# Raw weight pieces of the input and output projections loaded two pieces ahead of their split

## The chip, the cores and the metric

The kernel runs on one core of one Trainium2 chip. A core has TensorE (matmul; PE in the profile, its weight load PEld), VectorE (DVE), ScalarE (ACT), GpSimd (POOL) and SyncE (SP). Here SP only issues DMAs, and ScalarE issues some stores. Every engine works its own queue in order. The metric is the device time of one execution in microseconds, the median over several runs.

## What is computed

One encoder layer on x of 1024 tokens by 1024 features, in float32. The reference, cut to what matters:

```python
mod = cond @ w_ada[l] + b_ada[l]                    # cond = silu(c)
sh1, sc1, g1, sh2, sc2, g2 = jnp.split(mod, 6, axis=-1)
h = modulate(rms_norm(x, norm_mix_g[l]), sh1, sc1)
proj = h @ w_in[l]                                  # 1024 x 2832
q_a, k_a, v_a, qk_m, v_m, o_m, gates = jnp.split(proj, splits, axis=-1)
y_attn = axial_gqa_attention(q_a, k_a, v_a, ...)    # 8 heads of 64, 2 key/value heads
y_mem = bidirectional_mlstm(qk_m, v_m, o_m, gates, ...)  # 4 heads of 128, both directions
mix = jnp.concatenate([y_attn, y_mem], axis=-1) @ w_out[l]
x = x + g1[:, None, :] * mix
h = modulate(rms_norm(x, norm_ffn_g[l]), sh2, sc2)
x = x + g2[:, None, :] * ((jax.nn.silu(h @ w_gate[l]) * (h @ w_up[l])) @ w_down[l])
return rms_norm(x, final_norm_g)
```

## The kernel before, in words

Every large product keeps float32 accuracy by splitting both factors into a high and a low part: `whi` and `wlo` of a weight piece, `h_hi` and `h_lo` of the activations. `mm3` (line 311) makes one product of three matmuls: high by high (L312), one cross term (L313) and the other (L314).

**Weight pieces.** All weights that are used as they lie in memory pass through one list, `specs`, of pieces of about 256 KB (128 partitions by 512 columns). Pieces 0 to 11 belong to the first tiles: keys, values, first query tiles, first chunk tile. From piece 12 on come the tiles of the list `IN` (line 47), in that order: the third and fourth query tile (`q` 2 and 3, two pieces each), eight convolution tiles (`f`, two pieces each, weights `w_f`) and three chunk tiles (`t` 2, 1 and 3, four pieces each, weights `w_t`), up to piece 43. Pieces 44 to 75 are the output projection (`o` and `m`, one piece a unit, weights `w_o`), the list `MIX`. From 76 on come the gate and up projections (`w_gu`), and last the down projection.

**A piece's way.** A piece goes through three steps. `raw` (line 443) takes one of three `wst` buffers and issues the DMA on SP; it waits until the piece three before it has been split. `split` (line 461) makes `whi` by a copy on ScalarE and then `wlo` by a subtraction, on GpSimd for most pieces (VectorE for pieces 70 to 79 and a few others). The parts have six buffers each, so that the split of piece i must wait until the matmuls of piece i-6 are done. `load_piece` (line 488) is called once for every piece, when TensorE is done with a piece six before it: in query and convolution tiles (`tile_mms`, line 851) twice in the second half of a tile; in chunk tiles (`chunk_unit`, line 937) four times in the last of eight row blocks, one after the other; in the output projection (`out_unit`, line 1259) after each unit. Before the change it issues the piece's DMA and chains the split behind its arrival. In the down projection (`start["down"]` on) it issues the DMA of the piece `AHEAD` = 2 further on instead.

**Order.** The program is written out by a planner: `Clock` (line 127) runs a small model of the engines and of the DMA queue, chains wait for the times that this model expects, and streams of matmuls (`ck.streams`, line 215) are picked by readiness, main streams before fills. The order of the instructions on every engine is that of the model's time; on the chip each engine then waits for semaphores in that fixed order. SP's queue too is such an order: a store that waits for its data holds up the loads behind it.

**Stages around the change.** From about 84 us the pieces from 12 on are loaded. Up to about 160 us query, key and value tiles are finished: `rope_steps` (line 736) rotates a query tile with `sw` loads and stores it to `q_d`. Then the banks of PSUM are dealt out anew (line 2161) with a single one, `acc`, for the projection's tiles, and attention begins: `att_q` (line 1138) loads a head's queries (`qd`) and splits them (`qs`, low half on GpSimd), `scores` makes S (L1159), VectorE takes the row maximum (`sst`), ScalarE the exponential P, GpSimd the norm, TensorE turns P (L1191), ScalarE and VectorE split it (`PT`), and TensorE multiplies with the values (`av`, L1210). The convolution and chunk tiles fill TensorE between. A convolution tile's halves are evacuated by ScalarE (`xp`), VectorE applies five taps to them (`y`). GpSimd and ScalarE also work off the conditioning products (`ada`). At about 500 us attention ends, and the mLSTM begins (line 2194) with `mk`, `v` and `mq` loads, transposes (L1885, evacuated to `kt`) and `wv` on GpSimd; chunk tile 3 and then the output projection fill in. The gate and up projections begin at about 705 us.

Of the kernel before, what the change touches and what calls it, by code (L numbers as in the profile page):

```python
# [44 lines left out]
AHEAD = 2  # L45
# [204 lines left out]
def layer_kernel(ctx, tc, xT, c, w_ada, vecs, cons, rope, w_f, w_fT, w_t0, w_t, w_o, w_gu, w_d, out):  # L250
# [114 lines left out]
    with tc.manual_schedule():  # L365
# [62 lines left out]
        specs = [first[f][b] for b in range(2) for f in range(3)]  # L428
        start = {("t", 0): [6, 8, 9, 11], ("q", 1): [7, 10]}
# [31 lines left out]
        def split(p, delay, src, shape, *before, lo=None):  # L461

            def split_hi():
                p[0] = lined("whi", shape)
                act.activation(p[0], src(), AF.Copy)

            def split_lo():
                p[1] = lined("wlo", shape)
                (lo or gps).tensor_sub(p[1], src(), p[0].bitcast(F32))

            ck.chain(delay, *before, split_hi, split_lo, flag=p[2])

        made = []

        def piece(i):

            p = [None, None, Flag()]
            made.append((p, Flag(), []))
            if not isinstance(specs[i][0], str):
                src, n, ncol = specs[i][:3]  # L480

                def arrived(st, arrive):
                    made[i][2].append(st)
                    ck.chain(arrive, lambda: None, flag=made[i][1])

                raw([P, n, ncol], src, p[2], arrived)

        def load_piece():

            i = len(pieces)  # L490
            if i == len(specs):
                return
            while len(made) <= min(i + (AHEAD if i + AHEAD >= start["down"] else 0), len(specs) - 1):
                piece(len(made))
            p, there, st = made[i]
            pieces.append(p)
            if isinstance(specs[i][0], str):
                set_piece(p, *specs[i][1])
                return
            split(p, 0.0, lambda: st[0], [P, *specs[i][1:3]], there,  # L500
                  lo=dve if specs[i][3:] == (1,) or i < 9 or start["m", 2] <= i < start["b", 1] else None)
# [91 lines left out]
        def issue():  # L593

            kind, i = loads[0][0], int(loads[0][1:] or 0)
            del loads[0]
            if kind == "x":
                ck.chain(dma(x_t[i], xT[i]), lambda: None, flag=x_at[i])
            elif kind == "a":
                ada_load(i)  # L600
            else:
                load_piece()
            if loads:
                ck.at(max(0.0, ck.dma_t - 5.0 - ck.now), issue)
# [95 lines left out]
        for k in range(KT):  # L700
            if k < PES:
                for n in range(NH):
                    ck.need(sq_ok[k][n])
                    nc.tensor.matmul(msp[n][0], ones, by_pe[k, n], start=k == 0, stop=False)
                    ck.pe(0.86)
            for n in range(NH):
                ck.need(z_ok[k][n])
                for f in range(3):
                    mm3(acc0[f][n][0], weights([f, 3 + f], k, 4), (h_hi[k][:, halves(n)], h_lo[k][:, halves(n)]),
                        k == 0, k == KT - 1)  # L710
                    ck.pe(0.68)
            z_read[k].set(ck, ck.t)
            if k == 3:
                for _ in range(3):
                    load_piece()
            if k == 5:
                for n in range(NH):
                    ck.need(sq_ok[7][n])
                    ms = msp[n][0]
                    nc.tensor.matmul(ms, ones, ssx[n], start=False, stop=True)  # L720
                    ck.pe(0.86)
                    rstd_ok.append(rstd_steps(ms, 1.0 / D, f"n{n}", lambda y, n=n: rstd.__setitem__(n, y)))
                    y_ok.append(ck.chain(0.0, rstd_ok[n], lambda n=n: act.activation(msp[n][0], rstd[n], AF.Copy)))
                for n in range(NH):
                    for i in range(KT):
                        last.append(h_steps(n, i, *last[-3:-2]))
                h_ok = [last[0:KT], last[KT:]]
                ck.chain(0.0, *last[-3:], lambda: None, flag=y_free)
# [122 lines left out]
        def tile_mms(w0, last):  # L851

            for n in range(NH):
                for k in range(KT):
                    yield [pieces[w0 + k // 4][2]] + ([slot("acc")] if k == 0 else [])
                    if k == 0:
                        acc, f = psum_tile([P, HALF], "acc")
                        open_sum[0] = True
                    mm3(acc, weights(w0, k, 4), (h_hi[k][:, halves(n)], h_lo[k][:, halves(n)]), k == 0, k == KT - 1)
                    ck.pe(0.65)  # L860
                    if n == 1 and k % 4 == 3:
                        load_piece()
                    if k == KT - 1:
                        open_sum[0] = False
                        last(n, acc, f)
# [583 lines left out]
        def set_piece(e, p, i, m):  # L1449

            s = 2 * p + i
            R, Q = RAW[s], set_s[s]
            set_p[s][m] = e[2]
            eng = dve if p == 0 else gps
            done = lambda x: [set_p[s][x]] if x in set_p[s] else []
            sh = [P, 4, P]
            if m[0] == "A":
                split(e, 0.0, lambda: R[m[1:]][0], sh, R[m[1:]][1], lo=eng)
            elif m == "S2":
                split(e, 0.0, lambda: Q[2], sh, s2_ok[s], lo=eng)  # L1460
            elif m == "S3":
                split(e, 0.0, lambda: R["11"][0], sh, s2_ok[s], *done("A11"),
                      lambda: dve.tensor_sub(R["11"][0], R["11"][0], R["21"][0]), lo=eng)
            elif m == "S1":
                split(e, 0.0, lambda: Q[1], sh, s2_ok[s], lo=eng)
            else:
                split(e, 0.0, lambda: R["12"][0], sh, s2_ok[s], R["12"][1], *done("A12"),
                      lambda: dve.tensor_sub(R["12"][0], R["12"][0], Q[2]), lo=eng)
            if len(set_p[s]) == (7 if p >= NB else 5):
                ck.chain(0.0, *set_p[s].values(), lambda: None, flag=sets_done[s])  # L1470
                if s + 2 < 2 * NP:
                    ck.chain(0.0, sets_done[s], lambda: load_raws(s + 2))
# [844 lines left out]
```

## Time and profile before

| | us |
|---|---|
| median of 3 runs | 1377.88 |
| lowest and highest | 1376.33, 1381.36 |
| the profiled execution | 1373.45 |
| its span, first to last instruction | 1371.6 |
| TensorE busy | 1279.8 (93%) |
| VectorE busy | 1043.1 (76%) |
| ScalarE busy | 708.9 (52%) |
| GpSimd busy | 697.2 (51%) |
| DMA, mean over the span | 137 GB/s |

How to read the profile: a matmul's length overlaps with the next one's, so that the distance between two starts is what it costs. A row of a timeline has the start, the length, the engine, the line, the operation and `out<-in`, and, if the engine sat idle before it, in brackets for how long and what released it. Nearly all operations of DVE, ACT and POOL have the line of a recording helper, L98, and all DMAs of the helper `dma` L317, so that they are told apart by their tiles. A row of the waits has the waiter, the releaser, the total in us, how often, and the longest. Times are from the start of the span.

### The profile page before, as it was taken

To read this page: it belongs to the slowest core of one execution; us is meant where nothing else is said; L and a number is where in the kernel's file an instruction comes from. 1 tells how busy PE (TensorE), PEld (TensorE's weight loads), DVE (VectorE), ACT (ScalarE), POOL (GpSimd) and SP (SyncE) were. 2 spreads that over 40 slices of the span, in tenths; PEclk is the share of its full clock that TensorE was granted. 3 is DMA by queue.
4 is the path that set the end of the run, shared out by engine and by line. 5 is a ranking of instruction groups with operands and counts; after the bars stand their busy time and mean duration, and the time that the engine had idled before them with its cause. 6 is when DMAs were issued, how large, how long until landed. Compare 5 with 4: busy or idle time off the path is not lost.

```text
span 1371.6 us, 19596 instructions
## 1 busy us (share of the span) xinstructions
PE 1279.8 (93%) x6596; PEld 1074.1 (78%) x6596; DVE 1043.1 (76%) x1541; ACT 708.9 (52%) x1344; POOL 697.2 (51%) x580
## 2 busy tenths in 40 slices
PE   7889888899999979999999999999999999979997
PEld 5777677788778878877778788888888887857887
DVE  6937698975789748768698989877766654998876
ACT  6576366688577755454477522333333234344462
POOL 0353577655558436687605155545454455545542
PEclk9999999999999999999999999999999999989999
DMA  9444433233233146562553344332233159623324
GB/s 360 158 134 142 122 90 96 75 97 109 66 113 99 61 133 195 186 235 100 192 191 116 101 145 151 126 107 101 102 113 116 62 186 349 255 78 107 100 59 157
DMA packets 105044, 188.07 MB, mean 137 GB/s; under 512 B 11632, under 2 KB 33264, under 8 KB 104944
## 3 DMA queue, kind: packets, MB, share of 16 engines
q1 hardware_dynamic: 91552, 164.73, 37.6%
q10 hardware_dynamic: 13392, 22.10, 4.2%
q8 instruction: 52, 0.85, 0.3%
q14 instruction: 48, 0.39, 0.1%
HBM read 139.86 MB, written 43.25 MB: 133 GB/s over the span
## 4 chain that ended last, share of the span: by engine, by line
PE 55%; DVE 20%; issue 8%; ACT 6%; POOL 5%; DMA 4%; SPq 1%; DVEq 0%; ACTq 0%; POOLq 0%
PE acc L314 14%; PE acc L312 14%; PE acc L313 14%; DVE sst L98 3%; DVE y L98 3%; DVE x L98 2%; PE av L1210 2%; DVE PT L98 2%; PE T L1191 2%; PE S L1159 2%; POOL wlo L98 1%; DVE wd L98 1%; DVE s L98 1%; DVE Cs L98 1%; PE ni L1997 1%
## 5 line engine op out<-in xcount | busy, mean ns | idle before, releaser
L98 POOL TENSOR_TENSOR wlo<-wst,whi 128x512 fp32r<-128x512 f32 (+2 forms) x191 | 272.2, 1431 | 293.3 <-ACT whi L98 239.9
L98 ACT ACTIVATE whi<-wst 128x512 fp32r<-128x512 f32 (+2 forms) x223 | 133.1, 605 | 114.2 <-PE acc L314 27.6
L313 PE MATMUL acc<-x,whi 128*128 128x512 f32 x352 | 136.9, 389 | 0.0
L98 POOL TENSOR_SCALAR P<-P,sst 128x1024 f32<-128x1024 f32 x64 | 86.8, 1357 | 87.8 <-DVE sst L98 66.9
L98 POOL TENSOR_TENSOR wlo<-wr,whi 128x512 fp32r<-128x512 f32 x52 | 72.2, 1389 | 71.5 <-ACT whi L98 68.5
L312 PE MATMUL acc<-hh,whi 128*128 128x512 f32 x224 | 97.1, 433 | 7.7 <-ACT xp L98 6.2
L312 PE MATMUL acc<-whi,wch 128*128 128x512 f32 x244 | 96.8, 397 | 5.4 <-ACT wch L98 5.4
L314 PE MATMUL acc<-whi,wcl 128*128 128x512 f32 x244 | 96.8, 397 | 2.9 <-DVE wcl L98 2.8
L313 PE MATMUL acc<-wlo,wch 128*128 128x512 f32 x244 | 96.4, 395 | 0.2 <-POOL wlo L98 0.2
L98 ACT ACTIVATE P<-S,sst,colq 128x1024 f32<-128x1024 f32 x64 | 77.2, 1206 | 35.1 <-DVE sst L98 28.8
L98 DVE TENSOR_TENSOR PT<-T,PT 128x512 fp32r<-128x512 f32 x128 | 83.4, 681 | 9.3 <-ACT PT L98 9.1
L313 PE MATMUL acc<-hl,whi 128*128 128x512 f32 x224 | 90.0, 402 | 0.0
L314 PE MATMUL acc<-hh,wlo 128*128 128x512 f32 x224 | 89.8, 401 | 0.0
L98 ACT ACTIVATE whi<-wr 128x512 fp32r<-128x512 f32 x56 | 35.4, 632 | 100.2 <-DVE wr L98 49.1
L98 ACT ACTIVATE PT<-T 128x512 fp32r<-128x512 f32 x128 | 71.8, 596 | 28.6 <-PE T L1191 27.9
L1191 PE MATMUL T<-ident,P 128*128 128x128 f32 x512 | 72.2, 279 | 15.3 <-DVE PT L98 10.4
L312 PE MATMUL acct<-whi,hh 128*128 128x256 f32 (+1 forms) x256 | 81.6, 319 | 4.9 <-ACT hh L98 3.6
L98 DVE TENSOR_REDUCE sst<-S 128x1 f32<-128x1024 f32 x64 | 77.7, 1214 | 10.4 <-PE S L1159 8.9
L98 POOL TENSOR_TENSOR wlo<-s,whi 128x512 fp32r<-128x512 f32 x40 | 55.1, 1377 | 49.1 <-ACT whi L98 49.1
L1191 PEld LDWEIGHTS T<-ident,P 128*128 128x128 f32 x512 | 59.2, 143 | 25.9 <-issue 9.8
L98 POOL TENSOR_TENSOR ada<-ada,cond 128x512 f32<-128x512 f32 x48 | 68.1, 1419 | 21.9 <-DMA ada<-in_w_ada_dram 21.4
L98 DVE TENSOR_TENSOR wcl<-wd,wch 128x512 fp32r<-128x512 f32 x50 | 51.4, 1041 | 35.7 <-ACT wch L98 35.5
(486 smaller groups left out, 3853.9 us busy)
## 6 DMA issues: line engine op xcount, KB each, us to landing
wr<-in_w_gu_dram SPq DMA_DIRECT2D x66, 256.0 KB, 2.7
ada<-in_w_ada_dram SPq DMA_DIRECT2D x64, 256.0 KB, 3.3
wd<-in_w_d_dram SPq DMA_DIRECT2D x22, 512.0 KB, 6.4
wst<-in_w_gu_dram SPq DMA_DIRECT2D x42, 256.0 KB, 3.0
wst<-act_d SPq DMA_DIRECT2D x33, 256.0 KB, 4.2
ada<-in_w_ada_dram SPq DMA_DIRECT2D x16, 512.0 KB, 7.3
wst<-in_w_o_dram SPq DMA_DIRECT2D x32, 256.0 KB, 3.8
act_d<-sg ACTq DMA_DIRECT2D x29, 256.0 KB, 2.1
```

Of the source, the lines that this page charges most:

```text
L98: return fn(*args, **kw)
L312: nc.tensor.matmul(acc, w[0], x[0], start=first, stop=False)
L313: nc.tensor.matmul(acc, w[0], x[1], start=False, stop=False)
L314: nc.tensor.matmul(acc, w[1], x[0], start=False, stop=last)
L1159: nc.tensor.matmul(sp[:, halves(n)], qs[:, j * P:(j + 1) * P], k2[g][m][:, halves(n)], start=m == 0, stop=m == 1)
L1191: nc.tensor.transpose(tp[:, k], Pt[q][:, (4 * b + k) * P:(4 * b + k + 1) * P], ident)
L1210: nc.tensor.matmul(av, va[:, k, h // 4], PT[it][m][:, k], start=(k, m) == (0, 0), stop=(k, m) == (NJ - 1, 1))
L1997: nc.tensor.matmul(ni, x["q"][:, i * P:(i + 1) * P], H["Cs"][b][:, i4], start=True, stop=True)
```

## The change

One line of `load_piece` is replaced.

```diff
@@ -490,7 +490,8 @@
             i = len(pieces)
             if i == len(specs):
                 return
-            while len(made) <= min(i + (AHEAD if i + AHEAD >= start["down"] else 0), len(specs) - 1):
+            ahead = AHEAD if i + AHEAD >= start["down"] or start["q", 2] <= i < start["b", 0] - AHEAD else 0
+            while len(made) <= min(i + ahead, len(specs) - 1):
                 piece(len(made))
             p, there, st = made[i]
             pieces.append(p)
```

`start["q", 2]` is 12 and `start["b", 0]` is 76. So the calls for the pieces 12 to 73 now issue raw loads up to two pieces further on: the call for piece 12 issues 12, 13 and 14, each later one the piece two ahead, and the calls for 74 and 75 none. Each such load still waits in its chain for the one before it and for the split of the piece three before it, whose `wst` buffer it takes. The split of piece i is still chained at its own call. Nothing is added to what is computed.

## The prediction

> **What bounds the kernel now.** I read the page first, then the waits of the stretch that the change touches, then the busy times of pieces of that stretch, then the instructions around two holes in it.
>
> ```profile
> span 1371.6 us, 19596 instructions
> ...
> PE 55%; DVE 20%; issue 8%; ACT 6%; POOL 5%; DMA 4%; SPq 1%; DVEq 0%; ACTq 0%; POOLq 0%
> ```
>
> TensorE carries over half of the chain that ended last, VectorE a fifth, DMA 4%. A change to DMA issue can only pay where a late transfer opens a hole on TensorE or VectorE. The list of waits from 130 to 705 us (third query tile to the end of the output projection), engine, waiter, releaser, total, times, longest, has two rows that matter; the third is from the list for the whole span:
>
> ```profile
> ACT whi L98 <- DMA wst<-in_w_f_dram: 10.3, 2, 8.9
> POOL ada L98 <- DMA ada<-in_w_ada_dram: 21.4, 12, 3.0
> ACT whi L98 <- PE acc L313: 100.6, 66, 4.3
> ```
>
> So in the whole stretch ScalarE waits for a raw weight piece of `w_f` twice, 10.3 us, of which 8.9 us is one wait. The stretch in pieces (length; busy us of PE, PEld, DVE, ACT, POOL; granted clock; DMA share; GB/s):
>
> ```profile
> 156.60:161.40 4.80, 0.00 (x0) 0.00 (x0) 3.95 (x4) 1.11 (x2) 0.40 (x1) 0.93 0.95 227
> 161.40:167.10 5.70, 5.70 (x13) 4.45 (x14) 1.01 (x1) 4.44 (x6) 4.86 (x4) 0.50 0.20 52
> 171.00:300.00 129.00, 113.46 (x725) 99.60 (x724) 119.03 (x170) 91.82 (x183) 85.95 (x57) 0.97 0.33 93
> 300.00:500.00 200.00, 188.17 (x1245) 166.60 (x1244) 150.45 (x255) 140.53 (x277) 114.67 (x93) 1.00 0.27 83
> 496.90:501.50 4.60, 4.51 (x36) 4.38 (x36) 0.48 (x4) 1.31 (x2) 0.42 (x4) 1.00 0.59 174
> 501.50:505.70 4.20, 0.10 (x2) 0.06 (x1) 1.31 (x4) 1.41 (x2) 0.00 (x0) 0.97 0.97 322
> 505.70:512.80 7.10, 6.57 (x24) 5.30 (x24) 0.97 (x3) 4.91 (x11) 5.37 (x11) 0.54 0.82 279
> 512.80:705.00 192.20, 177.92 (x974) 149.56 (x975) 144.74 (x304) 101.21 (x242) 116.52 (x143) 0.99 0.54 178
> ```
>
> Two holes stand out: 4.8 us with no matmul before attention, and 4.2 us with two after it. Each is followed by a stretch at about half clock (0.50 for 5.7 us, 0.54 for 7.1 us). Between them attention is bound by VectorE (119 of 129 us), then by TensorE (188 of 200). Behind the second, TensorE is busy 178 of 192 us: there, work drawn into a hole is nearly time saved.
>
> **The change, part by part.** For pieces 12 to 75 the call that used to issue one DMA and chain its split now issues the DMA two pieces further on. Number and size of the DMAs, the three `wst` buffers and the splits stay. What moves: every raw load goes earlier in SP's queue by two calls; at the first call three go at once; every split follows its call without a DMA in between. The load of piece i+2 needs the buffer of piece i-1, so it waits for that piece's `wlo` on GpSimd. The last calls (74, 75) issue nothing.
>
> *Hole before attention.* The merged timeline (start, length, engine, what, idle before it and its releaser):
>
> ```profile
> 150.72 0.63 ACT L98 ACTIVATE whi<-wst 128x512 fp32r<-128x512 f32 x1
> 150.75 0.50 PE L312 MATMUL acc<-hh,whi 128*128 128x512 f32 x1 [0.69 <-ACT xp L98]
> ...
> 154.68 0.33 SPq L317 DMA_DIRECT2D q_d<-qg  x1
> 155.10 0.38 SPq L317 DMA_DIRECT2D wst<-in_w_f_dram  x1
> ...
> 156.09 0.39 PE L314 MATMUL acc<-hh,wlo 128*128 128x512 f32 x1
> ...
> 160.24 0.63 ACT L98 ACTIVATE whi<-wst 128x512 fp32r<-128x512 f32 x1 [8.88 <-DMA wst<-in_w_f_dram]
> 160.77 0.58 ACT L98 ACTIVATE xp<-acc 128x512 f32<-128x512 f32 x1
> 161.41 0.79 PE L312 MATMUL acc<-hh,whi 128*128 128x512 f32 x1 [4.92 <-ACT xp L98]
> 162.63 1.06 ACT L98 ACTIVATE qs<-qd 128x1024 fp32r<-128x1024 f32 x1 [1.28 <-DMA qd<-q_d]
> 164.32 2.37 POOL L98 TENSOR_TENSOR qs<-qd,qs 64x1024 fp32r<-64x1024 f32 x1
> 169.15 1.98 PE L1159 MATMUL S<-k,qs 128*128 128x512 f32 x8
> ```
>
> Piece 23's load (the 24th raw load on SP; pieces are counted from 0) stood in SP's queue behind the store of the last query tile, which left at 154.68. ScalarE, in order, sat 8.88 us on that split with the evacuation `xp` behind it, and TensorE, which has one accumulation bank there, sat 4.92 us behind `xp`. Issued two calls earlier, the piece is there by 151, `xp` runs at once and the second half starts about 157 instead of 161.41: 4.4 us. What is late next is the first score: it needs `qs`, whose low half ends on GpSimd at 164.32+2.37 = 166.69, and this hangs on the `qd` loads, which keep their place. So the score moves from 169.15 to 166.69 at best, 2.5 us. The idle time is not gone but moved in front of the score, and if the clock drops there as it did at 161.4, the eight score matmuls, about 0.23 us apart at full clock (24 matmuls from 150.75 to 156.09), go at 5.70/13 = 0.44: 1.7 us back, 0.8 left. I take **1.5 us**. Ends: 0, and 4.9 plus 13 x 0.21 = 7.6 if more matmuls were put ahead of the score.
>
> [...]
>
> *Hole after attention.* Same view:
>
> ```profile
> 499.78 0.43 SPq L317 DMA_DIRECT2D mk<-mqk_d  x1
> 500.89 1.87 SPq L317 DMA_DIRECT2D wst<-in_w_t_dram  x2
> 501.29 0.28 PE L314 MATMUL acct<-whi,hl 128*128 128x256 f32 x1
> 505.68 0.66 PE L1885 MATMUL tr<-ident,mk 128*128 128x128 f32 x2 [4.11 <-issue]
> 507.20 1.45 POOL L98 TENSOR_SCALAR wv<-v,cols 128x130 f32<-128x130 f32 x4 [7.69 <-DMA v<-v_d]
> 507.87 0.62 ACT L98 ACTIVATE whi<-wst 128x512 fp32r<-128x512 f32 x1
> 508.61 1.27 POOL L98 TENSOR_TENSOR wlo<-wst,whi 128x512 fp32r<-128x512 f32 x1
> 510.42 0.78 PE L312 MATMUL acct<-whi,hh 128*128 128x256 f32 x1
> 511.54 2.95 POOL L98 TENSOR_TENSOR wlo<-wst,whi 128x512 fp32r<-128x512 f32 x2 [0.23 <-ACT whi L98]
> ```
>
> At 501.29 chunk tile 3 stops in the middle of its first row block: pieces 40 and 41 are used, 42 and 43 were issued only at 500.89 and are split from 507.87 on. TensorE then waits for `mk`, the first load of the mLSTM. Changed, pieces 42 and 43 lie in SBUF since piece 41's call and are split while their predecessors' last block runs, on a GpSimd that was idle for 7.69 us. The 12 matmuls left (510.42 on) and the next block's 24 fit into the hole at 4.51/36 = 0.125 us each, the spacing just before it: 1.5 us for the 12 alone, 4.2 for the whole hole. How far the planner fills depends on when it believes `mk` to be there; I take 3. If the hole shrinks to about 1 us (after the 0.69 us at 150.75 the spacing stayed at 0.23) the half-clock stretch goes too: 6.57 us busy at 0.54 is 3.5 at full clock, at most 3.0 saved; but its matmuls also wait for `kt` and `wv`, so I take half, 1.5. The `wlo` behind the first `wv` (1.27 us) leaves GpSimd's queue there; I take 0.5 for that, at most 1.3. Together **5.0 us**, ends 1.5 and 8.5.
>
> *What it adds.* Before, no split from 130 to 705 us waited for TensorE, because the DMA took longer than the release of the `whi` buffer. Without it a split stands at ScalarE's head until the matmuls of piece i-6 are done, with exponentials, `PT` copies and evacuations queued behind it, and VectorE and TensorE behind those. The nearest price is the down projection, which already loads two ahead: 100.6/66 = 1.5 us a wait. Pieces 24 to 41 fall into attention, 18 x 1.5 = 27 us of ScalarE waiting against 129-92+200-141 = 96 us in which it idles there. I take **-0.5 us**; ends 0 and -14 (half of the 27 reaches VectorE).
>
> SP's queue: the 62 loads that now need a recent `wlo` hold whatever is behind them, the `ada`, `qd` and `mq` loads and the `ya_d` stores. Calls in attention mostly lie further apart than a split lasts, so I take 0; ends 0 and -5 (below). All orders after the first moved split are replanned, too; no row prices that. TensorE idles 11.8 us in 300 to 500 and VectorE 10 in 171 to 300; a quarter of both, 5 us to either side, is my estimate for its spread.
>
> Sum: 1.5 + 5.0 - 0.5 = **6.0 us**. The profiled execution took 1373.45 us (its span 1371.6 and 1.85 around it), so 1367.4 for such a one. It lies 4.43 below the median of the runs, 1377.88; from the median, **1371.9**. 0.5% is 6.9 us, about what a measurement of this kernel can tell from no change.
>
> **Rivals.**
> *More than this (1363).* Both holes close with their slow stretches: 7.6 + 8.5 - 0.5 = 15.6 at most, about 15. For it: both holes have the raw load as their last releaser or as the limit on what could fill them. Against: the first score needs `qs` at 166.69.
>
> *Nothing (1377).* The holes merely move and SP pays. A raw load waiting for GpSimd holds SP: the `wlo` of 42 to 44, from 508.61 to 511.54+2.95, come at 2 us each, and if five loads hold SP so long and half reaches GpSimd's `ada` products (which wait for DMA already, 21.4/12 = 1.8 us a time), 5 us of the 6 are gone. Against: SP is mostly idle ahead of stores. [...]
>
> *Slower (1386).* ScalarE's new wait for TensorE decides: 27 us in attention, half of it passed to VectorE, bound there, 14, against a gain of 6: 8 us slower. It decides from about 0.7 us a piece on, where half of 18 x 0.7 eats the 6. For it: ScalarE's queue is in order, as the 8.88 us show. Against: ScalarE has the slack.
>
> *It doesn't look ahead.* With three buffers the second piece ahead could wait for its buffer in a burst of calls, so that only part shows. Only the calls at a chunk tile's end come so fast; pieces 42 and 43 are called for long before. In with "nothing".
>
> **How the numbers follow.** Forecast (3 to 9 us faster) 0.42, more 0.19, nothing 0.23, slower 0.16. Of the forecast nearly half lies beyond 6.9 us: 0.20 + 0.19 = 0.39 faster; slower by over 6.9, 0.14; the rest, 0.47, same. Range: 1361 to 1385, which leaves out half of "more" and of the slower case. The likeliest case's own: 1369 to 1375.
>
> **What would show it.** Right: no `whi` wait for `wst<-in_w_f` over 1 us after 130 us; `xp` of that half at 157; the first score between 166 and 168; chunk tile 3 going on at 501 with no 4 us hole, and a clock near 1 behind it. The new wait: rows `whi` from PE in 130 to 705 us, under 20 us in total. Wrong: the first score still at 169, the 4.1 us wait for `mk` still there, `whi` from PE over 40 us, or attention longer than before by several us through a new order.

## The result, and the profile after

| | before | after |
|---|---|---|
| median, us (4 runs each, taken side by side) | 1377.57 | 1398.68 |
| lowest and highest, us | 1376.33, 1381.36 | 1396.95, 1401.62 |
| ratio after to before, 95% interval | | 1.0147 [1.0119, 1.0176] |
| the profiled execution, us | 1373.45 | 1400.16 |
| its span, us | 1371.6 | 1398.3 |

The change makes the kernel 21 us slower. I had forecast 6 us faster, and the range ended at 1385. The forecast was wrong, and the rival "slower" had given another reason than the one found below. First what the profile of the kernel after shows of the steps, then where the time went.

The page of the kernel after, span and chain:

```profile
span 1398.3 us, 19654 instructions
...
PE 60%; DVE 17%; issue 9%; ACT 5%; DMA 5%; POOL 4%; SPq 1%; DVEq 0%; POOLq 0%; ACTq 0%
```

Its list of waits from 130 to 705 us (waiter, releaser, total, times, longest):

```profile
POOL ada L98 <- DMA ada<-in_w_ada_dram: 30.2, 11, 8.3
...
PE ni L1998 <- DVE num L98: 23.0, 11, 11.7
ACT whi L98 <- PE acc L313: 22.8, 19, 2.7
...
ACT whi L98 <- DMA wst<-in_w_f_dram: 0.7, 1, 0.7
```

Two of my signs came as foretold. ScalarE's wait for raw pieces of `w_f` is gone (10.3 us, now 0.7), and its new wait for TensorE is 22.8 us in 19 waits, 1.2 us each, a little over the "under 20 us". A third row was not foretold: TensorE itself waits 11.7 us at one place, in the mLSTM. The busy times of stretches put it in place. The first three rows are the stretches of my two holes, the others stretches behind them. Kernel after:

```profile
156.60:161.40 4.80, 4.80 (x22) 3.71 (x20) 4.62 (x4) 0.18 (x1) 0.80 (x1) 1.00 0.81 211
161.40:167.10 5.70, 4.96 (x22) 3.86 (x21) 1.87 (x2) 2.32 (x3) 1.34 (x2) 1.00 0.63 144
...
500.00:520.00 20.00, 18.08 (x147) 17.55 (x146) 5.45 (x16) 8.84 (x17) 3.83 (x11) 1.00 0.65 207
...
540.00:550.00 10.00, 0.00 (x0) 0.00 (x0) 3.68 (x11) 0.38 (x2) 0.83 (x3) 0.50 0.58 183
550.00:560.00 10.00, 8.55 (x36) 7.54 (x37) 4.57 (x17) 1.92 (x6) 0.74 (x1) 0.62 0.53 157
640.00:700.00 60.00, 45.84 (x206) 35.77 (x205) 38.02 (x73) 24.67 (x54) 32.62 (x40) 0.89 0.33 103
```

The same view of the kernel before, for the stretches that were not shown:

```profile
500.00:520.00 20.00, 14.40 (x84) 12.70 (x83) 8.08 (x20) 11.38 (x25) 11.46 (x19) 0.83 0.75 240
...
540.00:550.00 10.00, 8.57 (x61) 7.68 (x59) 7.81 (x23) 6.03 (x18) 9.11 (x15) 1.00 0.72 219
...
640.00:700.00 60.00, 55.91 (x254) 44.73 (x253) 42.82 (x69) 30.82 (x56) 27.16 (x22) 1.00 0.46 150
```

Both holes that I had aimed at are closed, with the clock at 1.00 behind them. But from 540 to 550 us TensorE now does nothing at all, and from 640 to 700 us it is busy 10 us less than before. The instructions around the first of these, kernel after:

```profile
531.01 0.28 PE L314 MATMUL acct<-whi,hl 128*128 128x256 f32 x1
...
536.94 9.55 SPq L317 DMA_DIRECT2D ada<-in_w_ada_dram  x6
...
550.40 0.16 DVE L98 TENSOR_TENSOR mod<-modacc,vec 128x8 f32<-128x8 f32 x1
550.60 0.17 DVE L98 TENSOR_TENSOR mod<-mod,modacc 128x8 f32<-128x8 f32 x1
550.69 0.61 DVE L98 SCALAR_TENSOR_TENSOR num<-ni,cols,num 128x130 f32<-128x130 f32 x2
551.45 1.21 PE L1998 MATMUL ni<-Cs,mq 128*128 128x260 f32 x2 [11.66 <-DVE num L98]
```

The last matmul of chunk tile 3 (`acct`) is issued at 531. Then SP issues six loads of conditioning weights (`ada`) within 9.55 us, VectorE works them off and sums them into `mod`, and only then does the mLSTM go on. That is a place in the code that I had not priced, lines 2196 to 2199 of the kernel before:

```python
ck.streams(mem, [un], stop=lambda: un.wait is None and all(f.done for v in vo_ok for f in v))
while not summed:
    ck.need(*adas[-2:])
    ada_late(64)
```

`mem` is the mLSTM, `un` the stream of input tiles, whose last work is chunk tile 3. When that stream is used up, the planner stops the mLSTM too, and a loop follows that only takes the rest of the 64 late conditioning products, two in flight at a time. 16 of them are left for the mLSTM's beginning. How long they take, and how long chunk tile 3 lasts, decides. The loads of `ada` from 480 us on, before and then after (first and last start are the figures before the last dash):

```profile
L317 SPq DMA_DIRECT2D ada<-in_w_ada_dram x16: 327/333/825, 498.2 to 543.2; - x16
```

```profile
L317 SPq DMA_DIRECT2D ada<-in_w_ada_dram x16: 327/332/562, 506.0 to 546.2; - x16
```

And the first of the three matmuls of each chunk product (`acct`) behind the end of attention, before (from 497 us) and after (from 504.8 us):

```profile
L312 PE MATMUL acct<-whi,hh x72: 278/283/782, 497.0 to 568.7; 128*128 128x256 f32 x72
```

```profile
L312 PE MATMUL acct<-whi,hh x48: 278/283/472, 504.9 to 530.6; 128*128 128x256 f32 x48
```

Before, 72 products were left when attention ended (the last row block of chunk tile 1 and all eight of tile 3, 8 products each). They lasted until 568.7, far beyond the last `ada` load at 543.2, so that the loop found nothing to wait for. After, the weights came early enough for tile 1 to end sooner and for two row blocks of tile 3 to run inside attention. 48 were left, they ended at 530.6, and the `ada` loads at 546.2. The 24 products that moved cost TensorE 72 x 0.125 = 9 us, and attention's last store of results (`ya_d`) went from 496.96 to 504.85, 7.9 us later. So nothing was gained by moving them, and behind attention they were missing. This was one of the signs that I had named for being wrong: attention longer by several us through a new order.

The second loss, at 640 to 700 us, has a row in the list of TensorE's waits from 500 to 705 us, kernel after:

```profile
PE ni L1998 <- DVE num L98: 23.0, 11, 11.7
PE acc L312 <- ACT yah L98: 6.5, 1, 6.5
```

At 682 TensorE waits for the mLSTM's last output (`yah`), because the output projection has no other work ready. Before, that wait was 0.5 us.

### The profile page after: what moved, and what is told of

Read it like the earlier page. It is cut to its first block, busy times and chain, and to the rows that moved or that the text cites. A ratio compares the mean times of both kernels' runs of the same rounds, so it can differ in the third digit from the quotient of the medians.

```text
span 1398.3 us, 19654 instructions
## 1 busy us (share of the span) xinstructions
PE 1290.6 (92%) x6596; PEld 1081.1 (77%) x6596; DVE 1047.5 (75%) x1541; ACT 709.6 (51%) x1344; POOL 697.1 (50%) x580
## 4 chain that ended last, share of the span: by engine, by line
PE 60%; DVE 17%; issue 9%; ACT 5%; DMA 5%; POOL 4%; SPq 1%; DVEq 0%; POOLq 0%; ACTq 0%
PE acc L314 16%; PE acc L313 16%; PE acc L312 16%; DVE sst L98 3%; DVE y L98 3%; PE av L1211 3%; DVE PT L98 2%; PE T L1192 2%; PE S L1160 2%; POOL wlo L98 2%; DMA ada<-in_w_ada_dram 1%; DVE x L98 1%; PE ni L1998 1%; ACT P L98 1%; ACT PT L98 1%
## 5 line engine op out<-in xcount | busy, mean ns | idle before, releaser
L98 POOL TENSOR_SCALAR P<-P,sst 128x1024 f32<-128x1024 f32 x64 | 83.7, 1309 | 93.3 <-DVE sst L98 75.7
L98 POOL TENSOR_TENSOR ada<-ada,cond 128x512 f32<-128x512 f32 x48 | 71.3, 1487 | 30.6 <-DMA ada<-in_w_ada_dram 30.2
L314 PE MATMUL acct<-whi,hl 128*128 128x256 f32 (+1 forms) x256 | 75.0, 293 | 3.4 <-DVE hl L98 2.6
```

Source lines behind the costliest of these rows:

```text
L98: return fn(*args, **kw)
L314: nc.tensor.matmul(acc, w[1], x[0], start=False, stop=last)
```

## Experiments

Theory "drain" says: the raw loads do what they should, but the input stream is used up before the conditioning products are done, and the loop leaves TensorE empty. Its rivals: "ScalarE" (the splits' 22.8 us of waits for TensorE), "SP" (raw loads that wait for a buffer hold SP's queue), and, as it went on, "order" (any other order that the planner writes out costs this much). The medians, each beside runs of the kernel before on the same chip:

| run | look-ahead | other edit | us | before | ratio [95%] |
|---|---|---|---|---|---|
| e1 | all | mLSTM goes on | 1381.2 | 1377.52 | 1.0024 [1.0013, 1.0036] |
| e2 | input | | 1393.0 | 1377.52 | 1.0109 [1.0092, 1.0125] |
| e3 | to tile 1 | | 1372.89 | 1377.52 | 0.9970 [0.9951, 0.9989] |
| e4 | tile 3 | | 1396.93 | 1377.52 | 1.0146 [1.0127, 1.0165] |
| e5 | to tile 1 | mLSTM goes on | 1361.47 | 1376.28 | 0.9887 [0.9866, 0.9909] |
| e6 | input | mLSTM goes on | 1369.4 | 1376.28 | 0.9947 [0.9925, 0.9969] |
| e7 | all | 8 products earlier | 1393.61 | 1376.28 | 1.0120 [1.0098, 1.0141] |
| e8 | output | | 1384.61 | 1376.28 | 1.0060 [1.0039, 1.0080] |
| e9 | output | late splits | 1383.87 | 1375.97 | 1.0063 [1.0044, 1.0082] |
| e10 | to 35 | | 1399.63 | 1375.97 | 1.0172 [1.0150, 1.0193] |
| e11 | to tile 1, output | goes on, late splits | 1379.2 | 1375.97 | 1.0024 [1.0010, 1.0037] |
| e12 | output, by one | | 1383.02 | 1375.52 | 1.0052 [1.0038, 1.0065] |
| e13 | output | GpSimd's queue | 1396.23 | 1375.52 | 1.0144 [1.0128, 1.0161] |
| e14 | none | GpSimd's queue | 1388.6 | 1375.52 | 1.0098 [1.0079, 1.0117] |
| e15 | to tile 1, output by one | goes on | 1373.06 | 1375.52 | 0.9977 [0.9964, 0.9990] |
| e16 | output, by one | late splits | 1384.67 | 1376.39 | 1.0057 [1.0037, 1.0078] |
| e17 | none | later splits | 1382.88 | 1376.39 | 1.0054 [1.0036, 1.0071] |

### e1: the mLSTM goes on while the products are summed

```diff
-        ck.streams(mem, [un], stop=lambda: un.wait is None and all(f.done for v in vo_ok for f in v))
+        ck.streams(mem, [un], stop=lambda: un.wait is None and summed and all(f.done for v in vo_ok for f in v))
```

> The kernel after, but the mLSTM goes on until the conditioning products (ada) are summed, in place of a loop that only waits for them. Theory 'drain' (the input stream's work is used up by 531 instead of 569 us, and the loop that then drains the last ada products leaves TensorE empty for about 11 us at half clock): the hole of 540 to 551 closes, 8 to 14 us come back, about 1385 to 1391. Theory 'ScalarE' (splits wait 23 us for TensorE) and theory 'SP' (raw loads hold SP's queue, 42.7 us of waits for wlo): their waits stay, so 1396 to 1401, and what the hole gives is lost behind it. If the mLSTM's chain cannot use the time because its own latency bounds it: 1392 to 1398.

1381.2: 17.5 of the 21.1 us are back, more than the hole itself. The busy times of e1:

```profile
540.00:550.00 10.00, 9.05 (x53) 7.13 (x53) 8.73 (x28) 6.32 (x20) 7.84 (x13) 1.00 0.46 159
```

No other part of the change was undone, though the order behind the edit is a new one too, and ScalarE's waits for TensorE stayed (25.1 us from 130 to 730). "Drain" holds for most of the loss. The same edit brings 22.4 us on e2 and 10.2 us on e3, each taken against its own runs of the kernel before (e6 and e5 below), so that three different orders agree in the direction. In the kernel before, the same edit gives the same instructions in the same order on all engines: there the loop costs nothing.

### e2, e3, e4, e10: which look-ahead makes the hole

Only the range of the pieces differs, for example e3 (e2 ends at `start["o", 0] - AHEAD`, e10 at `start["t", 1] - AHEAD`, and e4 goes from `start["t", 3] - AHEAD` to `start["o", 0] - AHEAD`):

```diff
-            ahead = AHEAD if i + AHEAD >= start["down"] or start["q", 2] <= i < start["b", 0] - AHEAD else 0
+            ahead = AHEAD if i + AHEAD >= start["down"] or start["q", 2] <= i < start["t", 3] - AHEAD else 0
```

> Looks ahead in the input projections only (pieces up to 43, chunk tile 3 included); the output projection loads at its own calls, as before. 'Drain': the drain hole at 540 stays, nearly all of the loss stays, 1388 to 1400, and only what the output projection's own loads cost at the mLSTM's end (up to 8 us) can go. 'SP' and 'ScalarE' in the output projection: most of the 21 us go, 1378 to 1384.

> Looks ahead up to chunk tile 1 only (pieces up to 39); chunk tile 3 and the output projection load at their own calls. 'Drain': chunk tile 1 is still earlier by 5 us, but chunk tile 3 stops for its weights again in attention or behind it, so the stream reaches past 551 us or nearly, the hole at 540 is under 5 us, 1374 to 1386. 'ScalarE' in attention (18 pieces): the loss of attention, 8 us, stays, 1385 to 1390.

> Looks ahead for the four pieces of chunk tile 3 alone (40 to 43). 'Drain': attention is as before, the 4.1 us hole behind it closes with its slow clock (my 5.0 us), the stream still ends at about 560 us, behind the ada products: 1370 to 1375. If filling that hole only uses work up that is missing later: 1376 to 1381. 'SP' or 'ScalarE': little moves, 1376 to 1380.

> Looks ahead for the third and fourth query tile and the gate pieces only (up to 35), so for the hole ahead of attention and the first two thirds of attention; chunk tiles 1 and 3 and the output projection load at their own calls. My prediction's first term (1.5 us) less its new wait (0.5): 1373 to 1377 beside a before of 1376 to 1378. 'ScalarE' in attention: 1380 to 1386. If the gain of the short look-ahead (1372.9 against 1377.5) came from chunk tile 1, this is at 1375 to 1378; if from the gate pieces, at 1371 to 1374.

e2 came as "drain" expected. e3 came 1.1 us below its range, with a hole of 5.31 us where I had said under 5. e4 and e10 missed by over 20 us: I had thought that the weights of chunk tile 3 alone, or those up to chunk tile 2 alone (the "gate pieces" of the expectation for e10), would leave the end of the stream where it was. They do not. In both the planner draws row blocks of tile 3 into attention, which then ends at 509.5 and 509.1 (last `ya_d`), and the hole is there again. TensorE's rows behind the hole, e2, e3, e4 and e10 in this order:

```profile
551.37 1.21 PE L1998 MATMUL ni<-Cs,mq 128*128 128x260 f32 x2 [9.03 <-DVE num L98]
```

```profile
547.67 1.11 PE L2059 MATMUL tr<-ident,hs 128*128 128x128 f32 x4 [5.31 <-POOL hs L98]
```

```profile
558.82 1.21 PE L1998 MATMUL ni<-Cs,mq 128*128 128x260 f32 x2 [8.56 <-DVE num L98]
```

```profile
552.96 1.20 PE L1914 MATMUL U<-wv,kt 128*128 128x260 f32 x2 [15.12 <-DVE Cs L98]
```

The longest hole goes with how many chunk products are left behind attention, and so the end of the stream against the end of the `ada` loads (us):

| | left behind attention | last `acct` start | last `ada` load | longest hole of 530 to 560 | us |
|---|---|---|---|---|---|
| before | 72 | 568.7 | 543.2 | 1.84 | 1377.6 |
| e3 | 64 | 540.3 | 543.8 | 5.31 | 1372.9 |
| e4 | 50 | 539.2 | 554.4 | 8.56 | 1396.9 |
| e2 | 48 | 531.5 | 546.4 | 9.03 | 1393.0 |
| after | 48 | 530.6 | 546.2 | 11.66 | 1398.7 |
| e10 | 40 | 529.6 | 548.3 | 15.12 | 1399.6 |

In these six kernels, the fewer chunk products attention leaves, the longer the hole. In e3 attention ends as in the kernel before (497.2 against 497.0), all 64 products of tile 3 are left, and my hole at 501 is closed (TensorE busy 19.73 us of 500 to 520 against 14.40). There the change brings 4.6 us, near what I forecast, beside a hole that ends with GpSimd's `hs`. That the agreement is more than a lucky order is not shown: in e17 below, little but a new order is worth 6.5 us.

### e7: the products earlier

```diff
-        def ada_late(last=48, ahead=2):
+        def ada_late(last=56, ahead=2):
```

> The kernel after, with 8 of the last 16 conditioning products already taken in attention, the loop that drains them left as it was. 'Drain': 8 products are left for the mLSTM's beginning, about 20 us of the 40 that 16 took, so they end by 526 to 531 us, when chunk tile 3 ends; the loop finds nothing to wait for, and 10 to 16 us come back: 1382 to 1389, less what 8 products of some 0.7 to 1.2 us cost VectorE in attention. 'ScalarE' or 'SP': no more than 3 us come back, 1395 to 1399.

1393.61, 4 to 5 us back: too little for "drain" by its own numbers, too much for the rivals. The hole is 8.17 us where it was 11.66. Why no more came back was not shown. The direction fits, but the size shows nothing more.

### e5 and e6: without the hole

The edit of e1 on e3 and on e2.

> Looks ahead up to chunk tile 1 only, and the mLSTM goes on while the conditioning products are summed. 'Drain': the one hole that the short look-ahead still had (5.3 us without a matmul at 542) closes too, 3 to 6 us under the 1372.9 of the short look-ahead, about 1367 to 1370. If the early work of chunk tile 3 is only missing later, as filler for the mLSTM: 1371 to 1375.

> Looks ahead in all input projections but not in the output projection, and the mLSTM goes on while the conditioning products are summed. Between the full look-ahead with the same loop (1381.2) and this lies the output projection's look-ahead alone. If it costs what it cost without the loop's change (1398.7 - 1393.0 = 5.7 us): 1374 to 1377. If that cost came only from the drain: 1380 to 1382.

e5 is the best version: 1361.47, 14.8 us below the kernel before, and better than expected. The hole of e3 was 5.31 us, yet 11.4 came back. Most of the rest shows at the mLSTM's end. How much of the 14.8 us is a lucky order, no run shows. The stretch in e3 and then in e5:

```profile
640.00:700.00 60.00, 51.38 (x223) 40.73 (x222) 38.45 (x61) 29.05 (x52) 24.26 (x20) 0.94 0.43 141
```

```profile
640.00:700.00 60.00, 57.77 (x253) 46.09 (x252) 42.54 (x65) 35.75 (x59) 24.25 (x19) 1.00 0.52 173
```

e6 puts the output projection's own look-ahead at 1381.2 - 1369.4 = 11.8 us (10.6 with each run against its own kernel before), about twice what e2 gave (5.7).

### e8, e9, e11 to e17: what the output projection's look-ahead costs

e8 looks ahead there alone. e9 plans its splits 4 us after the call, so that they stand no earlier in ScalarE's queue while the loads stay early. e11 is e5 with this. e12, e15 and e16 look one piece ahead. e13 and e14 issue that projection's raw loads on GpSimd's queue, with and without look-ahead. e17 is the kernel before with these splits planned 5 us after their call. The edit of e9 (e17 has 5.0 for the 4.0, and e9 has the range of e8 beside it), and that of e13 and e14 (`raw` hands the queue on to `dma`; e13 has the range of e8 too):

```diff
-            split(p, 0.0, lambda: st[0], [P, *specs[i][1:3]], there,
+            split(p, 4.0 if start["o", 0] <= i < start["b", 0] else 0.0, lambda: st[0], [P, *specs[i][1:3]], there,
```

```diff
-                raw([P, n, ncol], src, p[2], arrived)
+                raw([P, n, ncol], src, p[2], arrived, nc.gpsimd if start["o", 0] <= i < start["b", 0] else None)
```

> Looks ahead in the output projection alone; the input projections load as before. 'SP' or 'ScalarE' there: 4 to 7 us slower than before, 1381 to 1385, with the mLSTM's end late as in the kernel after and waits of whi for TensorE only behind 580 us. If its cost came from the drain alone, which is not reached here: 1376 to 1379.

> Like the look-ahead in the output projection alone (1384.6, before 1376.3), but the split of each of its pieces is planned 4 us after its call, about where it stood when its load was issued at the call; the loads stay two pieces ahead. 'ScalarE' (the splits come so early that they stand at ScalarE's head until TensorE has freed the buffer, 15.3 us in 13 waits): these waits fall under 7 us and the 8 us come back, 1375 to 1379. 'SP' (the loads hold SP's queue, 8.6 us in one place): the loads stand as before and the loss stays, 1382 to 1387.

> The best so far (look-ahead up to chunk tile 1, the mLSTM going on, 1361.5), with the output projection's loads two pieces ahead as well but its splits planned 4 us after their call. 'ScalarE': the loads ahead cost nothing now, 1359 to 1364. 'SP': they hold SP's queue as in the other kernels, 1366 to 1371.

> Looks ahead in the output projection alone, by one piece in place of two. With three buffers a load one ahead needs the buffer of a piece whose low half is long made, so it seldom holds SP. 'SP': the waits of SP for wlo from 500 to 705 us fall from 30.4 towards the 8.2 of before, and the 8 us come back: 1374 to 1379. If the loss comes from the other order that any moved split makes: 1380 to 1388 with SP free.

> Looks ahead by two pieces in the output projection alone, and issues that projection's raw loads on GpSimd's queue, which makes most of the low halves itself and so waits little for them; SP is free of them. 'SP': 1374 to 1379, plus what issuing costs GpSimd (the control with the same queue and no look-ahead shows it). 'Order': 1382 to 1388.

> The control: the kernel before with the output projection's raw loads on GpSimd's queue, at their own calls. No theory of the change has a price for it; if GpSimd's issuing is cheap, as before, 1374 to 1379; if GpSimd is held by it, up to 1390.

> The best so far (1361.5) with a look-ahead of one piece in the output projection. 'SP': within 2 us of 1361.5, 1359 to 1364; 'Order': anything from 1361 to 1375, as the two-piece look-ahead with late splits gave 1379.

> Looks ahead by one piece in the output projection alone, with the split planned 4 us after the call: neither SP's waits for wlo nor ScalarE's for TensorE should be left (each run so far left one of the two). If 'SP' and 'ScalarE' each cost the 7 us when the other is gone: 1374 to 1378. 'Order' (another order of the mLSTM and its filler work is enough): 1380 to 1386 with both waits small.

> The kernel before, without any look-ahead, but the output projection's splits planned 5 us after their call, about 1 us later than their loads are believed to land: no wait is added or taken away, only the order changes (1,800 of TensorE's lines stand elsewhere). 'Order': 3 to 10 us off before in either direction, 1366 to 1373 or 1379 to 1386. If order alone is harmless: 1374 to 1378.

ScalarE falls as the only cause: in e9 its list has no wait of `whi` for TensorE from 560 to 705 us (15.3 in e8), and the time stays at 1383.87. So does SP: in e12 its waits for GpSimd's `wlo` over the same stretch are 9.4 us (28.3 in e8, 6.0 before), ScalarE's for TensorE 9.0, and it is still 7.5 us slower. With the loads off SP altogether the look-ahead costs 1396.23 - 1388.6 = 7.6 us. e16 was to remove both waits and did not: SP's are 24.7 there, because a later split is also a later `wlo`. e11 and e15, which add this look-ahead to e5, are about 18 and 12 us slower than e5, beyond every price that I had given for "ScalarE" and "SP". e17 comes nearest to a control of the order alone. It looks ahead nowhere, no `whi` on ScalarE waits for TensorE and TensorE waits for no weight piece from 500 to 705 us, and it is 6.5 us slower than the kernel before. But it is not quite alone: SP's waits for `wlo` are 11.8 us, 5.8 more than before. TensorE's waits of e17 from 500 to 705 us, and then of e16:

```profile
PE acc L312 <- ACT yah L98: 6.2, 1, 6.2
```

```profile
PE acc L312 <- ACT yah L98: 6.8, 1, 6.8
```

It is the row of the kernel after: at the mLSTM's end the projection has nothing ready but what hangs on the last head. In e5 there is no such row. e12 shows one way into it. Its rows at that place:

```profile
660.19 1.69 POOL L98 TENSOR_TENSOR wlo<-wst,whi 128x512 fp32r<-128x512 f32 x1
661.84 1.25 POOL L98 TENSOR_TENSOR hs<-hs,so 128x512 f32<-128x512 f32 x1
...
663.15 1.11 PE L2059 MATMUL tr<-ident,hs 128*128 128x128 f32 x4 [4.47 <-POOL hs L98]
```

A low half that now comes earlier stands ahead of the mLSTM's own `hs` on GpSimd, and TensorE waits 4.47 us. In the kernel before, `hs` ran at 660.76 and the low halves behind it, and TensorE waited 0.53. Open is how much of the 6 to 18 us that this look-ahead costs is such an order and how much SP's hold: no run looked ahead in this projection with both ScalarE's and SP's waits as small as before.

## Why the prediction was wrong, step by step

**The step that failed** is the sentence "Behind the second, TensorE is busy 178 of 192 us: there, work drawn into a hole is nearly time saved". It read a stretch of 192 us by its mean. In that stretch the mLSTM is a chain that leaves TensorE idle wherever no other work is ready, and it looked full only because chunk tile 3 and the output projection lasted just long enough. Work drawn ahead of the stretch was work taken from it: 72 products left became 48, and 1.84 us of longest hole became 11.66. The sum had no term for that. Undoing this consequence, in e1, gave back 17.5 of the 21.1 us.

**A second cost without a term** is the look-ahead in the output projection, pieces 44 to 75. With the mLSTM going on, the kernel with it is 3.7 us slower than the kernel before (e1), and without it 6.9 us faster (e6). That the 6.9 lies near my 6.0 is partly luck, since terms of the sum were off and little but a new order is worth as much. Why this look-ahead costs 10.6 us there stays open in part, as said above.

**The hole before attention** was mis-sized. It closed, and `xp` ran at 155.11 (I said 157). But the first score came at 169.47, not at 166 to 168, since `qs` had waited 3.17 us for `qd`, up to 165.36. I had the `qd` loads keep their place; the store `q_d` ahead of them left 1.6 us later than before (156.27 against 154.68). The time of the first score varies from kernel to kernel, with one profile of each: ten kernels with this look-ahead have their first score at 166.6 to 171.4, mean 168.9, nine without it at 168.4 to 170.8, mean 169.6. So the term is about 0.7 us, not 1.5, and with this spread it can't be told from nothing.

**The hole after attention** closed as forecast, with its half-clock stretch: the kernel after is busy 18.08 us of 500 to 520 where it was 14.40, at clock 1.00 where it was 0.83. As a term of the sum it counts only in e3, where no product of chunk tile 3 is drawn into attention: 4.6 us faster for both holes, beside my 6.0.

**The new wait on ScalarE** was 22.8 us in 19 waits, near "under 20 us", but that is luck in part. Up to 505 us there were 3 waits of 6.2 us, where the sum had 18 waits and 27 us; the other 16 stood in the output projection, for which it had none. The price of 1.5 us was also misread: 59 of the 66 waits of its row (87.2 of 100.6 us) lie between 705 and 1100 us, in the gate and up projections, which load at their own calls, and not in the down projection. My -0.5 was not shown wrong: no run removed the waits in attention, and e9 removed those in the output projection and gained nothing there. The rival "slower", which lived on it, had the right side for a wrong reason.

**SP's queue** at 0 stays unsettled: its waits for `wlo` from 130 to 705 us grew from 8.2 to 42.7 us, and no run separates them fully from the order.

**The reordering**, +-5 us by my estimate from idle time, was too small: e17, which does little but reorder, is 6.5 us off, and the 24 products drawn forward in the kernel after are a change of order, too. The idle shares from which I made the estimate were those of attention. The stretch that is sensitive to order lies behind it.

## What to carry to other kernels

A hole on the bounding engine is worth filling only with work that nothing later needs as cover: ask of every piece of work that moves forward what was hidden behind it, and compare the time at which that cover ends with the end of what it covers (here 568.7 against 543.2 us, a slack that the change used up). Look for loops in the program that wait without emitting other work, as they cost nothing until the work ahead of them runs out. And where a planner writes the order out, a change of a few us is judged beside a control that changes as little as it can but the order, and tried over several ranges, since here the same look-ahead gave -4.6, +15.5 or +23.7 us by the piece at which it ended (e3, e2, e10).

## What the runs showed of the hardware that was not expected

The clock fell behind a hole shorter than the two of 4.8 and 4.2 us that I had aimed at, and behind others of that length it did not. In the kernel before, TensorE stood idle for 1.84 us up to 556.50, and behind it came half clock:

```profile
554.00:556.00 2.00, 0.66 (x6) 0.45 (x4) 1.97 (x3) 0.37 (x1) 2.00 (x3) 1.00 0.00 0
556.00:558.00 2.00, 1.50 (x5) 1.35 (x6) 1.93 (x6) 0.00 (x0) 0.95 (x1) 0.66 0.00 0
558.00:560.00 2.00, 2.00 (x11) 1.85 (x10) 0.67 (x3) 1.00 (x2) 0.00 (x0) 0.50 0.20 66
```

The length of the hole alone did not decide it. At the same place of the program e12 stood idle for 2.18 us up to 557.43, and the clock was 1.00 from 558 to 560 us. In e16 it was 1.87 us up to 558.69, and the clock was 1.00 from 558 to 560 and from 560 to 580 us.

Behind the hole of 11.66 us in the kernel after, which ended at 551.45, TensorE was busy without a gap from 553 us on (2.00 of every 2.00 us up to 561). The clock was still 0.50 from 555 to 557 us, 3.6 to 5.6 us behind the hole's end, then 0.86 up to 559 and 1.00 up to 561 us.

Moving the 32 raw loads of the output projection from SP's queue to GpSimd's (e14) cost 13.1 us, though SP was rid of them. GpSimd spends 0.54 to 0.63 us on each of the 24 issues from 585 to 705 us (SP in the kernel before 0.33 to 0.69), and ScalarE waits 18.2 us in 11 waits from 500 to 705 us for the pieces to land, where it had waited 1.2 us once. How much of the 13.1 us is the other order was not separated.
